# A hybrid decoder layer on one core: three PSUM banks for the projection thirds, lower rank for the exponentials, B and C loaded first

## The chip, the cores and the metric

The kernel runs on one core of one Trainium2 chip. The metric is device time in microseconds (us): the median of the runs shown. The profile is one further execution, taken by the hardware profiler.

## The reference, cut to what matters

One layer: a Mamba-2 (SSD) mixer and a Gated DeltaNet (GDN) mixer read the same projection, then an output projection and a SwiGLU block follow, for 1024 prompt tokens and 8 sequences of 8 new tokens. The change lies in the SSD part: 16 heads of 64 channels, two groups of B and C of 128 states, a decay matrix of exponentials per head, and a gate silu(z).

```python
proj = h @ w_in
z, xbc, dt_raw, qkv, gate, beta_raw, alpha_raw = jnp.split(proj, ...)
xbc = jax.nn.silu(_causal_dwconv(xbc, ...))            # x, B, C
...
acs = jnp.cumsum(dtc * A, axis=2)
seg = acs[:, :, :, None] - acs[:, :, None, :]
decay_ls = jnp.exp(jnp.where(causal, seg, -jnp.inf))    # one matrix per head and chunk
cb = jnp.einsum("bclgn,bcsgn->bclsg", Cc, Bc)           # per group
y_diag = jnp.einsum("bclsgr,bcsgrp->bclgrp", cb[..., None] * decay_ls, xdt)
...                                                     # states from chunk to chunk, y_off
y = y + ssd_D[:, None] * xs
y = y * silu(z)                                         # then a norm per group
```

## The kernel before, in words

TensorE (PE) multiplies fp32 as three passes over high and low halves: a weight tile of 128 columns is cast to `wh` (ACT, L164) and `wl` (DVE, L165), and `gemm` issues 8 steps of L189, L190, L191. The tokens (1024 + 64) are cut in three, so a weight tile needs three products, each in one PSUM bank: these are the *thirds* (`third`). Between the steps of a third, `gemm` calls `tick()`, which lets generators that stand in line issue a few PE instructions of other work. PE's order is thus written out by the program and kept; the order on the other engines is set by a scheduler, by priority, and each engine then works in that order.

After the GDN stage comes the SSD stage, at about 750 to 1012 us. PE runs there the thirds of z tiles and x tiles, and between them the SSD work: `ssd_group` once per group g (transposes of B by L670, products of B and C by L1006 into `cb`), and `ssd_pair` once for each pair j of heads, eight in all. A third's bank comes from the pool `ps_a` (two banks), everything else on PE takes banks of `ps_b` (six). ACT empties a third's bank: `evac` of `silu_tile` (L613, L615) into `sz` for z, `evac` of `conv_raw` (L566, L568) into `raw` for x. The next third but one takes the same bank and waits for that.

`decays(j)` makes the two decay matrices of pair j, one tile `L` a head: a DMA (L1033, on the queue of SP), a mask on POOL (L1037), a subtraction on DVE (L1039), and on ACT 9 exponentials a head (L1042 x8 and L1043), in place. `ssd_pair(j)` calls `decays(j + 1)`, so the exponentials of a pair are issued while the pair before it is worked on. Then DVE multiplies `L` by `cb` (L1057), and PE uses it (L1106, L1145). In a pair DVE carries the state `hS` through the chunks (L1099), PE multiplies it by C (L1116), and ACT copies PSUM results that PE reads soon after (`hS`, L1109 and L1131) and scales the old states (`h0`, L1150). L593 is the Silu of an x tile. The Silu and the exponential need different tables on ACT, so a change from one to the other shows as ACT_TABLE_LOAD.

Before the first pair, `ssd_all` calls `decays(0)` and then `ssd_group(0)`, which loads `bT` (a tile of the name `eb`) and `cT` from DRAM:

```python
def ssd_all():
    L = decays(0)
    for g in range(2):
        grp = yield from ssd_group(g)
```

Of the kernel before, what the change touches and what calls it, by code (L numbers as in the profile page):

```python
# [8 lines left out]
F32 = mybir.dt.float32  # L9
F32R = mybir.dt.float32r  # L10
BF16 = mybir.dt.bfloat16
AF = mybir.ActivationFunctionType
# [4 lines left out]
P = 128  # L17
D = 1024
KD = D // P
NP = 1024  # L20
NS = 64
T = NP + NS
NB = 8
TS = 8
NC = NP // P
# [18 lines left out]
def hybrid_step(ctx: ExitStack, tc: tile.TileContext, x_p, x_s, c_p, c_s, st_ssd, st_ssdc, st_gdn, st_gdnc,  # L44
# [4 lines left out]
    pe, act, dve, pool, sp = nc.tensor, nc.scalar, nc.vector, nc.gpsimd, nc.sync  # L49
# [10 lines left out]
    ps_a = ctx.enter_context(tc.tile_pool(name="ps_a", bufs=2, space=PSUM))  # L60
    ph_q = ExitStack()
    ps_b = ph_q.enter_context(tc.tile_pool(name="ps_b", bufs=6, space=PSUM))
# [67 lines left out]
    def tick():  # L130
        clock[0] += 1
        for t in list(tasks):
            if next(t, tasks) is tasks:
                tasks.remove(t)

    def spawn(gen):
        tasks.append(gen)
# [5 lines left out]
    def wait(n):  # L143
        for _ in range(n):
            yield
# [11 lines left out]
    def bank():  # L157
        return bg[0].tile([P, 512], F32, name="ps")
# [26 lines left out]
    def gemm(out, wt, xh, xl):  # L185

        hi, lo = wt
        for k in range(KD):
            pe.matmul(out, lhsT=hi[k], rhs=xh[k], start=(k == 0), stop=False)  # L189
            pe.matmul(out, lhsT=hi[k], rhs=xl[k], start=False, stop=False)  # L190
            pe.matmul(out, lhsT=lo[k], rhs=xh[k], start=False, stop=(k == KD - 1))  # L191
            if k in (2, 5, 7):
                tick()
# [29 lines left out]
    bias = init.tile([P, 512], F32, name="bias")  # L223
# [7 lines left out]
    ps = bank()  # L231
# [218 lines left out]
    neg = cA.tile([P, NT, 24], F32, name="neg")  # L450
# [98 lines left out]
    for t in lcs:  # L549
        pool.memset(t, 0.0)  # L550

    def third(wt, g, evac):
        t0, n = TH[g]
        while g not in hid_box:
            tick()
        ps = ps_a.tile([P, 512], F32, name="ps")
        gemm(ps[:, 0:n], wt, [h[:, t0:t0 + n] for h in hh], [h[:, t0:t0 + n] for h in hl])
        evac(ps, t0, n, min(n, NP - t0))

# [12 lines left out]
    def conv_tile(wt, ti, taps, bias, dst, dp, ds_, ch, done=None):  # L572
# [3 lines left out]
        if done is None:  # L576
            for g in range(3):
                third(wt, g, evac)
# [32 lines left out]
    def silu_tile(wt, dst_p, dst_s):  # L611
        def evac(ps, t0, n, m):
            act.activation(out=dst_p[:, t0:t0 + m], in_=ps[:, 0:m], func=AF.Silu)  # L613
            if m < n:
                act.activation(out=dst_s, in_=ps[:, m:n], func=AF.Silu)  # L615

        for g in range(3):
            third(wt, g, evac)
# [39 lines left out]
            if i < 15:  # L658
                w4 = load(i + 1)


    pools = {}

    def four(t, a):
        return [t[:, (4 * a + i) * P:(4 * a + i + 1) * P] for i in range(4)]

    def flip4(srcs):
        ps = bank()
        for i, t in enumerate(srcs):
            pe.transpose(ps[:, i * P:(i + 1) * P], t, ident)  # L670
        return ps.rearrange("p (c n) -> p c n", n=P)
# [224 lines left out]
    def first_two(wts):  # L896

        raws = [conv_raw() for _ in wts]
        for ps, raw in zip(first_ps, raws):
            raw[2](ps, *TH[0], TH[0][1])  # L900
        for g in range(1, 3):
            for wt, raw in zip(wts, raws):
                third(wt, g, raw[2])
        ph_0.close()
        spawn(rates_done())
        for (_, run), raw in zip(pair, raws):
            run(None, raw)
# [76 lines left out]
    sqp = ph_c.enter_context(tc.tile_pool(name="sqp", bufs=1, reuse_waits="tile"))  # L984
    cv = ph_a.enter_context(tc.tile_pool(name="cv2", bufs=2, reuse_waits="tile"))
    sd = ph_a.enter_context(tc.tile_pool(name="sd", bufs=1, reuse_waits="tile"))
    rsg = const.tile([P, 2, NT], F32, name="rsg")
    pool.memset(rsg, 0.0)

    def ssd_group(g):  # L990
        bT = sd.tile([P, T], F32, name="eb", bufs=2)
        sp.dma_start(out=bT, in_=bcdr[g * P:(g + 1) * P, :])
        cT = sd.tile([P, T], F32, name="cT")
        sp.dma_start(out=cT, in_=bcdr[(2 + g) * P:(3 + g) * P, :])
        yield from wait(9)
        btk = sd.tile([P, NT, P], F32, name="btk")
        cb = sd.tile([P, T], F32, name="cb")
        for a in range(2):
            act.copy(btk[:, 4 * a:4 * a + 4, :], flip4(four(bT, a)))
            yield  # L1000
        pool.memset(cb[64:128, NP:T], 0.0)
        for a in range(2):
            ps = bank()
            for i in range(4):
                c = 4 * a + i
                pe.matmul(ps[:, i * P:(i + 1) * P], lhsT=bT[:, c * P:(c + 1) * P], rhs=cT[:, c * P:(c + 1) * P],  # L1006
                          start=True, stop=True)
            dve.tensor_tensor(out=cb[:, 512 * a:512 * a + 512].rearrange("p (c n) -> p c n", n=P),
                              in0=ps.rearrange("p (c n) -> p c n", n=P),
                              in1=tri.unsqueeze(1).to_broadcast([P, 4, P]), op=ALU.mult)  # L1010
            yield
        ps = bank()
        pe.matmul(ps[0:NS, 0:NS], lhsT=bT[:, NP:T], rhs=cT[:, NP:T], start=True, stop=True)
        pe.matmul(ps[0:NS, P:2 * P], lhsT=bT[:, NP:T], rhs=ident, start=True, stop=True)
        dve.tensor_tensor(out=cb[0:NS, NP:T], in0=ps[0:NS, 0:NS], in1=tri8[:, 0:NS], op=ALU.mult)
        act.copy(btk[0:NS, NC, :], ps[0:NS, P:2 * P])
        bb = sd.tile([NS, NB, P], F32, name="bb")
        dve.tensor_tensor(out=bb, in0=btk[0:NS, NC, :].unsqueeze(1).to_broadcast([NS, NB, P]),
                          in1=blkm.unsqueeze(2).to_broadcast([NS, NB, P]), op=ALU.mult)

        cz = halT[:, 12:22, :].rearrange("p i n -> p (i n)")[:, 0:224].rearrange("p (i n) -> p i n", n=56)
        pool.memset(cz, 0.0)
        for a in range(2):
            act.copy(cz[:, :, 32 * a:32 * a + TS],
                     cT[:, NP + 32 * a:NP + 32 * a + 32].rearrange("p (b t) -> p b t", t=TS))
        return cT, btk, cb, bb, cz

    def decays(j):

        L = []  # L1030
        for h in (2 * j, 2 * j + 1):
            t = sd.tile([P, T], F32, name="L", bufs=4)
            sp.dma_start(out=t, in_=accr[h, 0:T].partition_broadcast(P))  # L1033
            L.append(t)
        for h, t in zip((2 * j, 2 * j + 1), L):
            tc_ = t[:, 0:NP].rearrange("p (c n) -> p c n", n=P)
            pool.affine_select(out=tc_, in_=tc_, pattern=[[0, NC], [1, P]], compare_op=ALU.is_ge, fill=-1e30, base=0,  # L1037
                               channel_multiplier=-1)
            dve.tensor_scalar(out=t[:, NP:T], in0=t[:, NP:T], scalar1=acs[:, NC, h:h + 1], scalar2=0.0,  # L1039
                              op0=ALU.subtract, op1=ALU.min)  # L1040
            for c in range(NC):
                act.activation(out=tc_[:, c, :], in_=tc_[:, c, :], func=AF.Exp, bias=neg[:, c, h:h + 1])  # L1042
            act.activation(out=t[:, NP:T], in_=t[:, NP:T], func=AF.Exp)  # L1043
        return L

    def ssd_pair(j, L, grp, sqs):
        cT, btk, cb, bb, cz = grp
# [5 lines left out]
        sp.dma_start(out=h0, in_=st_ssd[0, :, 2 * j:2 * j + 2].rearrange("b h p n -> (h p) b n"))  # L1053
        box = sbox[j]
        box["next"] = decays(j + 1) if j + 1 < KD else None
        for t in L:
            dve.tensor_tensor(out=t, in0=t, in1=cb, op=ALU.mult)  # L1057
# [116 lines left out]
    def group_norm(g, sqs):  # L1174
        yield from wait(6)
        ps = bank()
        for c in range(NT):
            n = P if c < NC else NS
            pe.matmul(ps[0:n, c:c + 1], lhsT=sqs[:, c * P:c * P + n], rhs=ones[:, 0:1], start=True, stop=True)
        rsqrt_small(rsg[:, g, 0:NC], ps[:, 0:NC], 1.0 / 512, EPS)  # L1180
        rsqrt_small(rsg[0:NS, g, NC:NT], ps[0:NS, NC:NT], 1.0 / 512, EPS)
        if g == 1:
            rate_box["norm"] = clock[0]

    def ssd_all():
        L = decays(0)
        for g in range(2):
            grp = yield from ssd_group(g)
            sqs = sqp.tile([P, T], F32, name="sqs")
            for j in range(4 * g, 4 * g + 4):  # L1190
                yield from ssd_pair(j, L, grp, sqs)
                pairs[0] = j + 1
                L = sbox[j]["next"]
            spawn(group_norm(g, sqs))

    def run_z(j):
# [6 lines left out]
        return f  # L1203

    ssd_run = ssd_all()
    spawn(ssd_run)
    jobs = []
# [698 lines left out]
```

## Time and profile before

| | |
|---|---|
| median of 3 runs | 2038.79 us (2030.85 to 2044.51) |
| profiled execution, own time | 2044.61 us |
| its span | 2042.9 us |
| PE busy | 1967.6 us, 96% |
| DVE, ACT busy | 66%, 49% |
| mean granted clock of PE | 0.981 |

The span runs from the first to the last instruction of the profiled execution; 1.7 us of its time lie around it. PE is nearly always busy, so a change shows in the time by what it takes from, or adds to, PE's idle time and its stretches at the lower granted clock.

### The profile page before, as it was taken

Reading aid. Unit: us, or ns where it says so; the run is one execution under the profiler, and the core shown is the slowest. Engines: PE = TensorE matmul, PEld = TensorE weight load, DVE = VectorE, ACT = ScalarE, POOL = GpSimd, SP = SyncE. Lnnn points to the kernel's source line nnn. Section 1 sums busy time; section 2 is a strip of 40 time slices with the busy share of each in tenths; the row PEclk is TensorE's granted clock in tenths of the full one; section 3 lists DMA queues with packets and bytes.
Section 4 is the critical chain, followed back from the end, with each engine's and each line's share of the span. In section 5 each row is a group of like instructions: output and inputs, shape, how many; then the busy total and the mean of one; then the engine's idle time right before and its main releaser. Section 6 shows DMA issues by size and latency. Waiting matters only on the chain. (4 is left out here: it accounts for less than half of the span.)

```text
span 2042.9 us, 35462 instructions
## 1 busy us (share of the span) xinstructions
PE 1967.6 (96%) x13211; PEld 1766.5 (86%) x13211; DVE 1356.1 (66%) x2949; ACT 1009.6 (49%) x2511; POOL 136.3 (7%) x188
## 2 busy tenths in 40 slices
PE   6999999999999998999989999999999999999998
PEld 4888989999999998899856667899999999988886
DVE  4668777876887655767637777885555556645465
ACT  3545454655555446756423556753333334544454
POOL 2100000000000001010002210100000000000000
PEclk8899999999999999999989999999999999999999
DMA  9123332333221236545266856422222223643131
GB/s 306 44 63 98 92 103 89 109 96 101 83 57 56 67 98 185 158 125 153 93 207 187 260 176 223 135 79 75 80 74 78 76 80 111 223 143 109 49 99 49
DMA packets 224764, 239.49 MB, mean 117 GB/s; under 512 B 19128, under 2 KB 177387, under 8 KB 224461
## 3 DMA queue, kind: packets, MB, share of 16 engines
q1 hardware_dynamic: 218203, 231.88, 36.6%
q10 hardware_dynamic: 6386, 5.33, 0.8%
q8 instruction: 104, 1.70, 0.3%
q14 instruction: 71, 0.58, 0.1%
HBM read 190.93 MB, written 46.25 MB: 116 GB/s over the span
## 5 line engine op out<-in xcount | busy, mean ns | idle before, releaser
L189 PE MATMUL ps<-hh,wh 128*128 128x384 f32 (+1 forms) x1232 | 439.4, 357 | 7.2 <-ACT raw L568 3.0
L190 PE MATMUL ps<-hl,wh 128*128 128x384 f32 (+1 forms) x1232 | 405.9, 329 | 0.0
L191 PE MATMUL ps<-hh,wl 128*128 128x384 f32 (+1 forms) x1232 | 405.9, 329 | 0.0
L1327 PE MATMUL ps<-wh,sh 128*128 128x512 f32 x678 | 276.0, 407 | 7.7 <-ACT wh L164 7.0
L1330 PE MATMUL ps<-wl,sh 128*128 128x512 f32 x678 | 268.3, 396 | 4.7 <-DVE wl L165 4.6
L189 PEld LDWEIGHTS ps<-hh,wh 128*128 128x128 f32 x1232 | 234.1, 190 | 25.3 <-issue 10.4
L1329 PE MATMUL ps<-wh,sl 128*128 128x512 f32 x604 | 240.1, 398 | 0.0
L190 PEld LDWEIGHTS ps<-hl,wh 128*128 128x128 f32 x1232 | 234.4, 190 | 0.8
L191 PEld LDWEIGHTS ps<-hh,wl 128*128 128x128 f32 x1232 | 233.2, 189 | 0.0
L164 ACT CAST wh<-wr 128x512 fp32r<-128x512 f32 x200 | 123.7, 621 | 186.5 <-PE ps L190 90.5
L165 DVE TENSOR_TENSOR wl<-wr,wh 128x512 fp32r<-128x512 f32 x200 | 136.6, 687 | 65.5 <-ACT wh L164 64.9
L1327 PEld LDWEIGHTS ps<-wh,sh 128*128 128x128 f32 x678 | 129.0, 190 | 49.8 <-issue 12.3
L165 DVE TENSOR_TENSOR wl<-wd,wh 128x512 fp32r<-128x512 f32 x130 | 89.6, 692 | 117.5 <-ACT wh L164 114.2
L1330 PEld LDWEIGHTS ps<-wl,sh 128*128 128x128 f32 x678 | 129.1, 190 | 35.6 <-DVE wl L165 6.9
L164 ACT CAST wh<-wd 128x512 fp32r<-128x512 f32 x130 | 80.7, 621 | 138.4 <-PE ps L1329 100.5
L1329 PEld LDWEIGHTS ps<-wh,sl 128*128 128x128 f32 x604 | 115.5, 191 | 21.3
L1807 PE MATMUL ps<-T_0h,wh 128*128 128x272 f32 x352 | 103.5, 294 | 3.1 <-DVE u L1823 1.8
L1809 PE MATMUL ps<-T_0h,wl 128*128 128x272 f32 x352 | 103.4, 294 | 0.7 <-DVE wl L1745 0.7
L1744 ACT CAST wh<-s 128x512 fp32r<-128x512 f32 x104 | 64.3, 620 | 79.5 <-PE ps L1808 73.8
L1807 PE MATMUL ps<-T_1h,wh 128*128 128x272 f32 x352 | 102.2, 290 | 0.5 <-ACT as L1814 0.5
L1808 PE MATMUL ps<-T_0l,wh 128*128 128x272 f32 x352 | 102.7, 292 | 0.0
L1809 PE MATMUL ps<-T_1h,wl 128*128 128x272 f32 x352 | 101.6, 289 | 0.0
(490 smaller groups left out, 4383.3 us busy)
## 6 DMA issues: line engine op xcount, KB each, us to landing
wr<-in_w_in_dram SPq DMA_DIRECT2D x104, 256.0 KB
wr<-in_w_gate_up_dram SPq DMA_DIRECT2D x104, 256.0 KB
wr<-in_w_out_dram SPq DMA_DIRECT2D x96, 256.0 KB
w<-in_w_ada_dram SPq DMA_DIRECT2D x16, 1024.0 KB
wd<-in_w_down_dram SPq DMA_DIRECT2D x22, 512.0 KB
actdr<-as SPq DMA_DIRECT2D x18, 544.0 KB
L<-accr SPq DMA_DIRECT2D x16, 544.0 KB
am<-actdr SPq DMA_DIRECT2D x44, 192.0 KB
```

Source lines behind the costliest of these rows:

```text
L164: act.copy(wh, src)
L165: low.tensor_tensor(out=wl, in0=src, in1=wh.bitcast(F32), op=ALU.subtract)
L189: pe.matmul(out, lhsT=hi[k], rhs=xh[k], start=(k == 0), stop=False)
L190: pe.matmul(out, lhsT=hi[k], rhs=xl[k], start=False, stop=False)
L191: pe.matmul(out, lhsT=lo[k], rhs=xh[k], start=False, stop=(k == KD - 1))
L1327: pe.matmul(o, lhsT=sh[:, cs], rhs=wh, start=first, stop=False)
L1329: pe.matmul(o, lhsT=sl[:, cs], rhs=wh, start=False, stop=False)
L1330: pe.matmul(o, lhsT=sh[:, cs], rhs=wl, start=False, stop=last)
L1744: act.copy(wh, opa[p])
L1807: pe.matmul(o, lhsT=wh[:, cs], rhs=bh[:, m, :], start=(m == 0 and not on), stop=False, **on)
L1808: pe.matmul(o, lhsT=wh[:, cs], rhs=bl[:, m, :], start=False, stop=False, **on)
L1809: pe.matmul(o, lhsT=wl[:, cs], rhs=bh[:, m, :], start=False, stop=(m == 3), **on)
```

## The change

Three edits, all in the SSD stage. (1) `third` counts its calls, and once the SSD pools exist every third call takes its bank from `ps_b`. (2) The exponentials of `decays(j)` for j > 0 are issued at a lower priority: 40 lower for the first head of a pair, 120 lower for the second. (3) The loads of `bT` and `cT` become a function, `load_bc`; for group 0 it is called ahead of `decays(0)`. `pools` only moves up. All lines below shift by 3 to 8: L613 becomes L616, L615 L618, L566 L569, L568 L571, L593 L596, L1042 L1048, L1043 L1049, L1109 L1115, L1131 L1137.

```diff
+    pools, thirds = {}, [0]
+
     def third(wt, g, evac):
         t0, n = TH[g]
         while g not in hid_box:
             tick()
-        ps = ps_a.tile([P, 512], F32, name="ps")
+        thirds[0] += 1
+        ps = (ps_b if "ssd" in pools and thirds[0] % 3 == 0 else ps_a).tile([P, 512], F32, name="ps")
         gemm(ps[:, 0:n], wt, [h[:, t0:t0 + n] for h in hh], [h[:, t0:t0 + n] for h in hl])
         evac(ps, t0, n, min(n, NP - t0))
...
     sd = ph_a.enter_context(tc.tile_pool(name="sd", bufs=1, reuse_waits="tile"))
+    pools["ssd"] = sd
...
-    def ssd_group(g):
+    def load_bc(g):
         bT = sd.tile([P, T], F32, name="eb", bufs=2)
         sp.dma_start(out=bT, in_=bcdr[g * P:(g + 1) * P, :])
         cT = sd.tile([P, T], F32, name="cT")
         sp.dma_start(out=cT, in_=bcdr[(2 + g) * P:(3 + g) * P, :])
+        return bT, cT
+
+    def ssd_group(bT, cT):
         yield from wait(9)
...
-            for c in range(NC):
-                act.activation(out=tc_[:, c, :], in_=tc_[:, c, :], func=AF.Exp, bias=neg[:, c, h:h + 1])
-            act.activation(out=t[:, NP:T], in_=t[:, NP:T], func=AF.Exp)
+            with tc.high_priority(-(40 + 80 * (h % 2)) if j else 0):
+                for c in range(NC):
+                    act.activation(out=tc_[:, c, :], in_=tc_[:, c, :], func=AF.Exp, bias=neg[:, c, h:h + 1])
+                act.activation(out=t[:, NP:T], in_=t[:, NP:T], func=AF.Exp)
         return L
...
     def ssd_all():
-        L = decays(0)
         for g in range(2):
-            grp = yield from ssd_group(g)
+            bc = load_bc(g)
+            if g == 0:
+                L = decays(0)
+            grp = yield from ssd_group(*bc)
```

PE and POOL keep their order. On the queue of SP the two loads go ahead of the two first `L`, as the diff shows, and one weight load later moves by a place. What else moves is on ACT, and behind it on DVE. Three places follow.

ACT, at the start of the stage, while pair 0 begins: `ps_8836`, `ps_8883` and `ps_8983` are the three thirds of one z tile, read into `sz_8835`; `L_8924` and `L_8926` are the decay matrices of pair 1, heads 0 and 1. Before:

```order
L999 COPY btk_8846<-ps_8863 128x512
L613 ACTIVATE sz_8835<-ps_8836 128x384
L1024 COPY halT_124<-cT_8732 128x4x8 x2
L1016 COPY btk_8846<-ps_8908 64x128
L1042 ACT_TABLE_LOAD
L1042 ACTIVATE L_8924<-L_8924,neg_644 128x128 x8
L1043 ACTIVATE L_8924<-L_8924 128x64
L1042 ACTIVATE L_8926<-L_8926,neg_644 128x128 x8
L1043 ACTIVATE L_8926<-L_8926 128x64
L613 ACT_TABLE_LOAD
L613 ACTIVATE sz_8835<-ps_8883 128x384
L613 ACTIVATE sz_8835<-ps_8983 128x256
```

And now:

```order
L616 ACT_TABLE_LOAD
L616 ACTIVATE sz_8835<-ps_8836 128x384
L1021 COPY btk_8846<-ps_8908 64x128
L616 ACTIVATE sz_8835<-ps_8883 128x384
L164 CAST wh_9012<-wr_9010 128x512
L1049 ACT_TABLE_LOAD
L1049 ACTIVATE L_8924<-L_8924 128x64
L1048 ACTIVATE L_8924<-L_8924,neg_644 128x128 x8
L616 ACT_TABLE_LOAD
L616 ACTIVATE sz_8835<-ps_8983 128x256
L618 ACTIVATE sz_8835<-ps_8983 128x64
```

The reading of `ps_8883` has moved ahead of all exponentials of pair 1, that of `ps_8983` ahead of the second head's, and there is one table load more.

ACT, at the end of pair 2: `ps_9711` is the last third of an x tile, read into `raw_9572`; `L_9766` and `L_9768` belong to pair 4. Before:

```order
L164 CAST wh_9842<-wr_9840 128x512
L1171 ACTIVATE sz_9301<-y_9599 128x1088
L1042 ACT_TABLE_LOAD
L1042 ACTIVATE L_9766<-L_9766,neg_644 128x128 x8
L1043 ACTIVATE L_9766<-L_9766 128x64
L1042 ACTIVATE L_9768<-L_9768,neg_644 128x128 x8
L1043 ACTIVATE L_9768<-L_9768 128x64
L566 COPY raw_9572<-ps_9711 128x256
L568 COPY raw_9572<-ps_9711 128x8x8
```

And now:

```order
L164 CAST wh_9842<-wr_9840 128x512
L1177 ACTIVATE sz_9301<-y_9599 128x1088
L569 COPY raw_9572<-ps_9711 128x256
L571 COPY raw_9572<-ps_9711 128x8x8
L586 ACTIVATE xs_9827<-raw_9572,prm1T_122 128x1024
L588 ACTIVATE xs_9827<-raw_9572,prm1T_122 128x64
L600 COPY lc0_646<-raw_9572 128x3
L601 COPY lc0_646<-raw_9572 128x24
L164 CAST wh_9848<-wr_9846 128x512
L1048 ACTIVATE L_9766<-L_9766,neg_644 128x128 x8
```

The two copies from the bank have moved ahead of the exponentials of pair 4.

ACT, in pair 5: `hS_10760` and `hS_10792` are copies that PE reads, `L_10559` a matrix of the pair after, `xs_10638` an x tile under its Silu. Before:

```order
L164 CAST wh_10659<-wr_10657 128x512
L1109 COPY hS_10706<-ps_10707 128x512
L613 ACT_TABLE_LOAD
L613 ACTIVATE sz_10663<-ps_10664 128x384
L1150 ACTIVATE h0_10555<-h0_10555,eb_10552 128x128
L1122 COPY y_10683<-ps_10697 128x128
L1150 ACTIVATE h0_10555<-h0_10555,eb_10552 128x128 x7
L1109 COPY hS_10760<-ps_10761 128x512
L1131 COPY hS_10792<-ps_10783 128x128
L593 ACTIVATE xs_10638<-xs_10638 128x1024
```

And now:

```order
L1048 ACTIVATE L_10559<-L_10559,neg_644 128x128
L1128 COPY y_10683<-ps_10697 128x128
L1048 ACTIVATE L_10559<-L_10559,neg_644 128x128 x3
L1049 ACTIVATE L_10559<-L_10559 128x64
L1156 ACTIVATE h0_10555<-h0_10555,eb_10552 128x128 x7
L1115 COPY hS_10760<-ps_10761 128x512
L596 ACT_TABLE_LOAD
L596 ACTIVATE xs_10638<-xs_10638 128x1024
L597 ACTIVATE xs_10638<-xs_10638 128x64
L1137 COPY hS_10792<-ps_10783 128x128
```

Exponentials now stand among the pair's own work, and a table load and the Silu of `xs` have come between the two copies.

## Rows read from the trace of the kernel before

**Rows 1.** The page's first part: busy time of each engine, whole span.

```profile
PE 1967.6 (96%) x13211; PEld 1766.5 (86%) x13211; DVE 1356.1 (66%) x2949; ACT 1009.6 (49%) x2511; POOL 136.3 (7%) x188
```

**Rows 2.** Waits of PE, 750 to 1012 us: total, times, longest, in us.

```profile
PE ps L189 <- ACT raw L568: 3.0, 1, 3.0
PE ps L670 <- DMA eb<-bcdr: 3.0, 1, 3.0
PE ps L189 <- ACT sz L613: 2.8, 2, 2.6
PE ps L189 <- ACT sz L615: 1.3, 1, 1.3
```

**Rows 3.** Timeline of PE around three stops: start, length, instruction, idle before it.

```profile
768.67 0.66 PE L670 MATMUL ps<-ident,eb 128*128 128x128 f32 x4 [3.00 <-DMA eb<-bcdr]
...
773.82 1.05 PE L1006 MATMUL ps<-cT,eb 128*128 128x128 f32 x8
...
788.22 0.44 PE L189 MATMUL ps<-hh,wh 128*128 128x384 f32 x1 [2.62 <-ACT sz L613]
...
790.90 0.33 PE L1106 MATMUL ps<-L,xd 128*64 128x128 f32 x2
...
861.20 0.34 PE L190 MATMUL ps<-hl,wh 128*128 128x384 f32 x1
861.38 0.34 PE L191 MATMUL ps<-hh,wl 128*128 128x384 f32 x1
864.73 0.45 PE L189 MATMUL ps<-hh,wh 128*128 128x384 f32 x1 [3.02 <-ACT raw L568]
...
866.08 0.52 PE L191 MATMUL ps<-hh,wl 128*128 128x384 f32 x1
866.40 0.52 PE L189 MATMUL ps<-hh,wh 128*128 128x384 f32 x1
```

**Rows 4.** Busy time (count) by window: PE, PEld, DVE, ACT, POOL; clock; DMA share.

```profile
768.60:773.20 4.60, 4.53 (x20) 4.43 (x21) 0.00 (x0) 4.57 (x13) 0.00 (x0) 0.63 1.05 296
...
788.20:798.00 9.80, 9.78 (x85) 9.19 (x86) 5.86 (x19) 3.79 (x11) 0.00 (x0) 1.00 0.20 55
...
864.70:868.50 3.80, 3.77 (x15) 3.77 (x16) 1.89 (x2) 3.77 (x7) 0.00 (x0) 0.58 0.18 54
...
750.00:1010.00 260.00, 249.86 (x1831) 229.79 (x1830) 175.93 (x358) 158.69 (x393) 21.15 (x25) 0.99 0.47 139
```

**Rows 5.** Timeline of ACT ahead of the stops that end at 788.22 and 864.73.

```profile
780.00 1.28 ACT L1042 ACT_TABLE_LOAD   x1
781.29 2.45 ACT L1042 ACTIVATE L<-L,neg 128x128 f32<-128x128 f32 x8
...
786.39 1.28 ACT L613 ACT_TABLE_LOAD   x1
787.68 0.77 ACT L613 ACTIVATE sz<-ps 128x384 f32<-128x384 f32 x2
...
864.22 0.35 ACT L566 COPY raw<-ps 128x256 f32<-128x256 f32 x1
```

**Rows 6.** Timeline of SP's queue: the first loads of the stage.

```profile
760.46 1.66 SPq L1033 DMA_DIRECT2D L<-accr  x2
762.17 0.42 SPq L992 DMA_DIRECT2D eb<-bcdr  x1
```

**Rows 7.** Timeline of DVE: the first work on each of the two first `L`.

```profile
764.51 1.18 DVE L1039 TENSOR_SCALAR L<-L,rate 128x64 f32<-128x64 f32 x1 [0.95 <-DMA L<-accr]
767.36 1.19 DVE L1039 TENSOR_SCALAR L<-L,rate 128x64 f32<-128x64 f32 x1 [1.67 <-DMA L<-accr]
```

**Rows 8.** Timeline of ACT and of DVE inside pairs 5 and 2.

```profile
951.48 0.27 ACT L1131 COPY hS<-ps 128x128 f32<-128x128 f32 x1 [0.74 <-PE ps L1128]
951.64 1.06 ACT L593 ACTIVATE xs<-xs 128x1024 f32<-128x1024 f32 x1
...
846.50 1.62 DVE L1099 SCALAR_TENSOR_TENSOR hS<-hS,rate,ps 128x64 f32<-128x64 f32 x8 [1.32 <-PE ps L1085]
```

More of the change, by code (lines that the diff above doesn't have):

```diff
@@ L659, in ada_rest @@
                 w4 = load(i + 1)
-    pools = {}
     def four(t, a):
```

## The prediction

> **What bounds the kernel now.** I read the page's first part first: PE is busy for 1967.6 us, 96%, while DVE stands at 66% and ACT at 49% [rows 1]. So an edit on ACT or on a queue is worth only what it takes out of PE's idle time, or out of its time at the lower clock. The edits touch one stage, 750 to 1012 us, so the second view is the list of PE's waits there [rows 2]. It holds four lines: 3.0 us for a copy into `raw`, 3.0 us for the load of `eb` (this is `bT`), 2.8 us in two waits for a Silu into `sz`, 1.3 us for another. Together that is 10.1 us, and it is all that PE waits there by the trace. The window of the whole stage bounds it from the other side: PE is busy for 249.86 of 260 us [rows 4], which leaves 10.1 us too.
>
> The third view is PE's timeline around the stops [rows 3], and beside it the granted clock [rows 4]. After the stops that end at 768.67 and at 864.73 the chip grants 0.63 of full speed over 4.6 us and 0.58 over 3.8 us, a mix of its two levels, 2.4 and 1.2 GHz. In PE's rows this is a start every 0.32 us (866.08, 866.40) where it had been one every 0.18 us (861.20, 861.38). After the stop that ends at 788.22, 2.62 us long, the clock stays at 1.00. The lost time is 4.6 x (1 - 0.63) = 1.7 us and 3.8 x (1 - 0.58) = 1.6 us, together 3.3 us. A stop that goes takes its slow stretch with it, so the **ceiling** of the change is 10.1 + 3.3 = 13.4 us, 0.7% of the time.
>
> The fourth view tells whose work stands in front [rows 5]. Ahead of the stop that ends at 788.22, ACT has loaded the table for the exponential (1.28 us), done two heads (2.45 us for eight), and loaded the table back (1.28 us), before it reads the bank at 787.68. Ahead of the stop that ends at 864.73 it does the same two heads of another pair, as the order at the second place shows, and copies the bank only at 864.22. In both cases PE had ended its third and needed the bank but one.
>
> **Part by part.** *Three banks.* With two banks a third waits for the reading of the third before the last; with three, every third third starts in a bank that has long been free, and the others wait for one read earlier. Following the bank of each third through the order after, the ones that start behind the stops for `sz` and `raw` take banks that were last read before the exponentials in front of them, or that DVE had read well before. The Silu waits (2.8 and 1.3) and the `raw` wait (3.0) go by this alone: 7.1 us, with the 1.6 us of clock behind 864.73. The price would be an SSD step that finds one of its six banks still held by a third. Those steps come at the earliest some microseconds after ACT's reading; I put it at nothing, and the cover is ACT's promptness: if a reading comes late, PE waits at the SSD step for the same copy.
>
> *Lower rank.* It takes the same waits from the other side, since copies now go ahead of the exponentials of the next pair (the order at the first and second places). So the first two edits overlap, and their gain counts once. What rank does alone is to move exponentials into the pair's own work. They are needed only a pair later: those of pair 1 begin at 781.29 before [rows 5], while PE first reads even pair 0's at 790.90 [rows 3], so their own lateness costs little at first. The cost lies in ACT's order, which is fixed: a copy that PE waits for directly can now stand behind a table load and exponentials. Before, no such wait shows in this stage in any line of [rows 2], so one place at a time has to be bounded. At least 0 (the exponentials fit into a gap of ACT, which is busy for only 158.69 of 260 us [rows 4]), and at most a table load and a head, 1.28 + 2.45 = 3.7 us [rows 5], in each of seven pairs: 26 us. By place: in pair 5 the copy into `hS` that began at 951.48 now stands behind a table load and the Silu that came after it (1.28 + 1.06 = 2.3 us) [rows 5, 8]; I take half, about 1.2 us, since the copy waited 0.74 us for PE anyway and PE reads it some time after its end. In pair 2 the second head's exponentials end, by adding their lengths up in ACT's gaps, near 846; DVE's product with `cb` follows, and the eight updates of the state that began at 846.50 [rows 8] move behind it: about 1.0 us. In pair 3 about 0.3 us, in the others nothing. Sum 2.5 us, near the lower end since most places have a gap in front.
>
> The change adds four table loads on ACT. By the row one takes 1.28 us, and the next activation starts 0.01 us after its end (781.29 behind 780.00 + 1.28) [rows 5]: 4 x 1.28 = 5.1 us of ACT, of an idle time of 260 - 158.69 = 101 us in the stage. I count it inside the places above and nowhere else. The Trainium skill, page "ScalarE: Activation LUTs", section "What ACT_TABLE_LOAD costs", speaks against this edit: it gives a switch of tables about 2.66 us, the load of 1283 ns and a drain of some 1380 ns. By it the four would be an estimated 10.6 us of ACT. The trace agrees on the load; no row here shows a drain behind it.
>
> *B and C first.* PE stops for 3.00 us, up to 768.67, for `bT`, the third load in the queue, issued at 762.17 behind the two `L` [rows 3, 6]. The first two landed at 764.5 and 767.3 by the work that DVE starts on them [rows 7]. Now `bT` is first and `cT` second, in the same slots and of the same size, so they should land at 764.5 and 767.3. PE wants `bT` at 768.67 - 3.00 = 765.7: no wait, by a margin of 1 us. Without the stop and the slow stretch it wants `cT` 4.7 us earlier than the 773.82 at which it multiplied by it [rows 3], at 769.1: a margin of 1.8 us. The gain is 3.0 + 1.7 = 4.7 us. The price is that the two `L` of pair 0 land about two loads later, by an estimate from `bT`'s 768.67 as third near 768.7 and 771. Their exponentials take twice 2.45 us and a table load [rows 5], so they end near 778, and DVE's product of the second head near 780. PE reads them first at 790.90, or near 783.6 without the stops up to there (3.00 + 1.7 + 2.62): some 3 us of slack. What is late next is the reading of a z third behind these exponentials (the table load and `ps_8836` at the first place), near 778; the third that takes its bank is the one that starts at 788.22 before, near 781 without the stops.
>
> **The sum.** 7.1 + 1.6 + 4.7 = 13.4 us, less 2.5 us: **11 us**. The profiled execution of 2044.61 us, span 2042.9 and 1.7 around it, would become 2033.6. It lies 5.8 us above the median of the runs, so I take the gain off the median: 2038.79 - 11 = **2028 us**. Behind the stage PE's order is the same, and the queues there wait for events of PE and DVE that come earlier with it, so the gain is kept.
>
> **The rivals.** *Most of it eaten on ACT.* The four table loads all stand in front of copies that PE waits for: 4 x 1.28 = 5.1 us more, so 13.4 - 2.5 - 5.1 = 6 us, **2033**. For it: ACT's order is fixed, and pair 5 shows the pattern. Against: ACT idles 101 us in the stage. By the page's price the four cost 10.6, and with 2.5 the gain would be nothing, **2038.5**; no row bears that out, and I give it 0.03 apart from the above.
>
> *Slower.* The copies of `hS` that PE reads at once stand behind a table load and a head's exponentials in every pair: 3.7 us x 7 = 26 us, less 13.4: +12.6 us, **2051**. It decides from 13.4 / 7 = 1.9 us a pair on. For it: the exponentials now run among the pair's own steps, where DVE, ACT and PE hand work to each other with waits under 1 us. Against: at seven places out of seven a whole head would have to start just ahead of a copy; the order shows the exponentials split around the copies, and only one place with a load between two of them.
>
> *It does nothing.* `bT` lands no earlier since the weight and state loads share the DMA engines (busy share 1.05 behind 768.6 [rows 4]), and a third stops for another reading: gain under 2 us, **2038**. Against: the first load in the queue had landed 4 us after its issue.
>
> *More than expected.* Without stops the clock stays up in places that I don't count, or the stage's end meets less idle time behind it: over 20 us, under 2018. No row in the stage has that much to give.
>
> **Chances.** Forecast (gain of 7 to 14 us) 0.62, eaten on ACT 0.17, the page's price 0.03, nothing 0.06, slower 0.06, more 0.06. The range holds the forecast, the eaten gain and the case of nothing, and on either side some 5 us for the runs themselves, which spread by 14 us before: 2017 to 2042. A measurement of this kernel tells about 1% (20 us) from no change, and the ceiling is 0.7%, so: faster by over 1% 0.06, within 1% 0.89, slower by over 1% 0.05 (the slower case, with its price nearly doubled or unlucky runs).
>
> **What would show it.** In the profile after, PE's list of waits between 750 and 1012 should have lost the lines of `raw`, `eb` and `sz`, and the window around 768 and 865 should show a clock of 1.00. New lines of PE waiting for `hS` or DVE waiting for `L` should sum to 2 to 3 us. If `eb` is still there, the step on the landing of the first load is wrong; if a third still waits for `sz` or `raw`, the step on the banks; if PE waits for `hS` in most pairs, the price of the rank was too low. The stage's end, near 1012 us before, should come some 11 us earlier, and PE's busy time be less by the 3.3 us of slow clock.

## The result, and the profile after

The changed kernel takes 2021.78 us, median of 10 runs (2017.53 to 2033.8), against 2037.61 (2030.85 to 2050.06) for the kernel before: a ratio of 0.9922, 95% interval 0.9906 to 0.9937, so some 16 us less (13 to 19). A second comparison, on another occasion (run c1 below), gave 0.9935 (0.991 to 0.996), 13 us. The forecast was 11 us and 2028, in a range of 2017 to 2042.

The profiled execution after has a span of 2015.8 us. PE is busy for 97% of it, 96% before [rows 1], and for 16.3 us less:

```profile
PE 1951.3 (97%) x13211; PEld 1752.5 (87%) x13211; DVE 1356.6 (67%) x2949; ACT 1014.1 (50%) x2515; POOL 138.7 (7%) x188
```

Only 2.0 of these 16.3 us are in the stage (271.4 us before and 269.4 after). 10.0 lie ahead of it, in code that is the same, and are clock: the mean granted clock up to the stage is 0.97 in the trace before and 0.99 in this one. So the busy time that the forecast named as a sign can't be read from these two traces.

PE's waits after, 750 to 1012 us (total, times, longest), answer to [rows 2]:

```profile
PE ps L1091 <- DVE xe L1074: 3.0, 1, 3.0
PE ps L1286 <- POOL rsg L122: 0.9, 1, 0.9
PE ps L1141 <- ACT hS L1137: 0.9, 2, 0.7
PE ps L1122 <- DVE hS L1105: 0.2, 1, 0.2
```

All four lines of before are gone: `raw`, `eb` and both of `sz`. (The wait for `rsg` lies behind the pairs, in the part that the stage's end has moved into the window.) In their place stands one that no step of the forecast has: 3.0 us for `xe`. PE's timeline after shows the stop, and the windows what the clock did behind it (columns as in [rows 4]):

```profile
773.31 0.34 PE L191 MATMUL ps<-hh,wl 128*128 128x384 f32 x1
776.66 1.14 PE L1091 MATMUL ps<-xe,btk 128*128 128x128 f32 x8 [3.02 <-DVE xe L1074]
```

```profile
756.00:762.00 6.00, 6.00 (x42) 5.92 (x41) 0.91 (x3) 1.96 (x7) 0.27 (x1) 1.00 0.91 288
...
776.60:782.00 5.40, 5.34 (x35) 4.91 (x36) 5.37 (x15) 5.35 (x14) 1.09 (x1) 0.68 0.54 145
848.00:852.00 4.00, 4.00 (x37) 3.71 (x36) 4.00 (x8) 3.95 (x10) 0.07 (x1) 1.00 0.89 283
...
750.00:1010.00 260.00, 255.77 (x1882) 232.58 (x1881) 183.49 (x372) 168.07 (x408) 23.15 (x26) 0.99 0.52 153
```

The first window is where PE multiplies by `bT` now, the third where it used to stop for `raw`: full clock in both, where [rows 4] have 0.63 and 0.58. The second is the stretch behind the new stop, at 0.68: 5.4 x 0.32 = 1.7 us more. So of the 3.3 us of clock in the forecast's ceiling this trace kept half.

PE runs the same instructions in the same order in both kernels, so the lead of one trace over the other can be read at each of them (its start before less its start after). Between the products that stand at 760 and at 784 us before, the lead grows by 4.9 us (the stop for `bT` with its slow stretch); over the stop that ended at 788.22 it grows by 2.8; between 788 and 800 it falls by 4.7 (the new stop); then come 1.6 for the second Silu wait and 4.9 for the `raw` wait with its slow stretch; between 950 and 990 it falls by 1.6. Over the stage that makes 8.2 us in these two traces.

The lead over the whole execution, 27.1 us, is not all the change's: 8.3 us of it are there before the stage begins, in code that is the same. The runs below give such a split for every kernel.

### The profile page after: what moved, and what is told of

Its sections match the earlier page's. It is cut to its first block, busy times and chain, and to the rows that moved or that the text cites. A ratio compares the mean times of both kernels' runs of the same rounds, so it can differ in the third digit from the quotient of the medians.

```text
span 2015.8 us, 35469 instructions
## 1 busy us (share of the span) xinstructions
PE 1951.3 (97%) x13211; PEld 1752.5 (87%) x13211; DVE 1356.6 (67%) x2949; ACT 1014.1 (50%) x2515; POOL 138.7 (7%) x188
## 4 chain that ended last, share of the span: by engine, by line
PE 79%; DVE 9%; DMA 6%; ACT 3%; issue 2%; POOL 0%; SPq 0%; DVEq 0%; POOLq 0%; ACTq 0%
PE ps L189 8%; PE ps L190 8%; PE ps L191 8%; PE ps L1815 7%; PE ps L1817 7%; PE ps L1816 7%; PE ps L1335 7%; PE ps L1338 6%; PE ps L1337 6%; PE ps L671 2%; PE ps L725 1%; DMA L<-accr 1%; DVE tm L827 1%; DVE rr L829 1%; DMA mx<-mixdr 1%
## 5 line engine op out<-in xcount | busy, mean ns | idle before, releaser
L1337 PEld LDWEIGHTS ps<-wh,sl 128*128 128x128 f32 x604 | 114.7, 190 | 21.3
```

The source lines that it names most:

```text
L1337: pe.matmul(o, lhsT=sl[:, cs], rhs=wh, start=False, stop=False)
```

## The experiments

All are compared with the kernel before. Beside each ratio, what the stage took in the trace: from the start of one given product to that of another (at 733.5 and 1015.2 us in the first trace of before), and what the execution had before these and after them, up to the end of its last product.

```
kernel                                   ratio (95%)             before it  stage  after it
before, first trace                                                  733.5  281.7  1020.7
c0  before again                         1.0004 (0.9985-1.0023)      725.3  285.5  1016.0
the change                               0.9922 (0.9906-0.9937)      725.2  273.5  1010.0
c1  the change again                     0.9935 (0.991-0.996)        731.8  272.2  1017.4
e1  three banks only                     0.9943 (0.9919-0.9967)      731.4  276.5  1015.6
e2  lower rank only                      0.9932 (0.9908-0.9956)      731.9  275.0  1014.9
e3  B and C first only                   0.9978 (0.9961-0.9995)      730.1  278.9  1016.6
e6  rank, B and C first                  0.9959 (0.9941-0.9977)      725.6  277.4  1010.6
e5  banks, B and C first                 0.9916 (0.9896-0.9936)      730.5  269.6  1010.7
c2  e5 again                             0.9929 (0.9913-0.9944)      726.1  274.5  1015.7
e4  change, subtraction ranked lower     0.9912 (0.989-0.9934)       726.7  271.3  1015.9
e9  e5, subtraction ranked lower         0.9927 (0.9908-0.9945)      732.7  268.9  1016.1
e7  change, L of pair 1 loaded earlier   0.9907 (0.9892-0.9923)      725.3  269.4  1015.3
e8  e5, L of pair 1 loaded earlier       0.9906 (0.9885-0.9928)      725.0  268.5  1015.0
```

The columns beside the stage spread by 8.5 and 10.7 us between traces, without regard to the edits. The stage's own column sorts by them better and is read first below, but two traces of one program differ there too, by 3.8 us (before), 1.3 (the change) and 4.9 (e5 and c2). A stage by itself is known to some 2 us, and differences of 1 or 2 us between kernels show nothing.

Part of that spread is the clock. Summed over the stage (length times one less the granted clock), the time lost to it is 3.4 us in the first trace before and 6.8 in c0; 1.7 in both traces of the change, in e5, c2 and e9; 3.4 in e1, e2 and e6; 5.1 in e3; nothing in e4, e7 and e8. Not every slow stretch follows a stop. Here are c1 and the first trace before over the same products, with no wait of PE near by:

```profile
882.70:886.10 3.40, 3.40 (x13) 3.31 (x12) 1.17 (x1) 2.70 (x7) 1.71 (x2) 0.50 0.22 64
```

```profile
896.70:900.10 3.40, 3.40 (x23) 3.36 (x23) 1.78 (x5) 2.62 (x8) 2.58 (x2) 1.00 0.33 87
```

The granted clock falls to 0.50 at this place (the lower of its two levels, 1.2 GHz) in c0, c1, e1, e3, e5, e6 and e9 and stays up in the other seven traces, whatever the edits; it costs up to 1.7 us. Nor does every stop have one: in c0 a slow stretch follows the stop that [rows 4] show at full clock.

**The two controls.** c0 is the kernel before, unedited.

> The kernel before once more, to see by a second trace how much its own executions differ outside the stage. The stage from 760 to 1012 us should show the same four waits of PE, 10 us in all, whatever the time. In the first trace what follows the stage took about 5 us longer than in three of the four variants, whose code is the same there. If that was chance, it is gone in this trace; if it stays, the variants gain something behind the stage too. Ratio 1.000.

Ratio 1.0004. The four waits are there, but that for `eb` is 4.1 us in place of 3.0, and the stage takes 3.8 us more than in the first trace; what follows it takes 4.7 less. Beside the longer wait it is the two more slow stretches (3.4 us) that make c0's stage the longer one. So the stage before is 283.6 us, give or take 2, and the 5 us behind it were largely chance.

c1 is the changed kernel, unedited.

> The changed kernel once more: ratio 0.992 again. In its stage PE waits 3 us for xe again (the cause is in the order and in the loads), and the stage is some 8 us shorter than in the kernel before. What follows the stage, 10.6 us shorter than before in the first pair of traces, comes out 4 to 6 us shorter, or less, if that was chance.

The stage takes 272.2 us, 11.4 less than the mean of the two of before (10.1 in the first trace of the change). The wait for `xe` is 1.2 us and not the 3.0 expected, with the same program and no slow stretch behind it: the stop depends on when a load lands, not on the order alone.

```profile
PE ps L1091 <- DVE xe L1074: 1.2, 1, 1.2
```

What follows the stage is 3 us shorter than in the first trace of before, and 1.4 longer than in the second: the 10.6 us were chance for the most part.

**One edit at a time.** e1 has the banks alone:

```diff
+    pools, thirds = {}, [0]
...
+        thirds[0] += 1
+        ps = (ps_b if "ssd" in pools and thirds[0] % 3 == 0 else ps_a).tile([P, 512], F32, name="ps")
...
+    pools["ssd"] = sd
```

> The three banks alone, without the lower rank and without B and C first. By my theory (the waits for sz and raw go by the banks alone) PE's list of waits from 750 to 1012 us loses the lines of sz (2.8 and 1.3 us) and raw (3.0), keeps the 3.0 of eb, and the clock behind the raw wait (1.6) comes back: 8.7 us less than before, a ratio of 0.9957. The rival (the rank does it, a third bank only moves the wait to a later third, as the exponentials still stand in front of the copy) has at least 4 us of waits for sz and raw left and a gain of under 4 us, 0.998 or more.

e2 has the rank alone:

```diff
+            with tc.high_priority(-(40 + 80 * (h % 2)) if j else 0):
                 for c in range(NC):
                     act.activation(out=tc_[:, c, :], in_=tc_[:, c, :], func=AF.Exp, bias=neg[:, c, h:h + 1])
                 act.activation(out=t[:, NP:T], in_=t[:, NP:T], func=AF.Exp)
```

> The lower rank alone, with two banks and with the old order of loads. By my theory the copies out of the banks go ahead of the exponentials, so the waits for sz and raw go as they do with three banks, against 2.5 us of new waits for hS and L: 6 us less than before, 0.997. The rival (with two banks a third still starts before ACT has come to the copy, and the additional table loads stand in front of it) gives a gain of under 2 us, or a loss: 0.999 to 1.002.

PE's waits in the stage, of e1 and then of e2 (L671 is L670 of before; line numbers move by 1 to 8 in the changed kernel, not by 3 to 8):

```profile
PE ps L671 <- DMA eb<-bcdr: 4.1, 1, 4.1
PE ps L1121 <- DVE hS L1104: 1.1, 2, 0.6
PE ps L1140 <- ACT hS L1136: 0.2, 1, 0.2
```

```profile
PE ps L671 <- DMA eb<-bcdr: 3.5, 1, 3.5
PE ps L1141 <- ACT hS L1137: 0.9, 2, 0.7
PE ps L189 <- ACT sz L616: 0.2, 1, 0.2
```

Each edit by itself takes away the waits for `sz` and `raw`, but for 0.2 us: the stage is 7.1 us (banks) and 8.6 us (rank) shorter than before. Both rivals fall. The two gains are the same one, as the forecast had it. (By its ratio e2 gained more than the 6 us expected, 0.9932 against 0.997; part of that is the excess over the stage that is taken up below.) Without the rank PE waits for the state `hS` instead, which no step had: in e1 1.1 us, in pairs 0 and 2. The rank's price in PE's waits is 0.7 us, for the copy in pair 5; the other 0.2 of that line are at 1013.6 us in the trace before as well, just outside [rows 2].

e3 has the loads alone, with `ssd_group(g)` split into `load_bc(g)` and the rest as in the diff of the change:

```diff
     def ssd_all():
-        L = decays(0)
         for g in range(2):
-            grp = yield from ssd_group(g)
+            bc = load_bc(g)
+            if g == 0:
+                L = decays(0)
+            grp = yield from ssd_group(*bc)
```

> B and C first alone. By the sum on record the stop for eb and its slow stretch go: 4.7 us, 0.9977. The rival comes from the trace after the change: without that stop the loads of the pair after next go out earlier and share the DMA engines with the matrices L of pair 1, DVE waits for these ahead of xe, and PE for xe (3.0 us and about 1.7 of clock): gain of 0 to 1 us, 1.000 to 0.9995, with a line of PE waiting for xe in its place.

```profile
PE ps L189 <- ACT raw L571: 3.0, 1, 3.0
PE ps L189 <- ACT sz L616: 1.2, 2, 1.0
PE ps L189 <- ACT sz L618: 1.2, 1, 1.2
PE ps L1090 <- DVE xe L1073: 0.9, 1, 0.9
```

The wait for `eb` is gone and the stage 4.7 us shorter. That it is just the term of the sum is partly chance: in PE's waits e3 saves the 3.0 us and another 1.7 of the Silu waits (2.4 in place of 4.1), pays 0.9 for `xe`, and loses more to the clock than the first trace before (5.1 and 3.4 us). Its ratio, 0.9978, is the one expected. The rival has its wait too, 0.9 us for `xe`, but not its price.

**Two edits at a time.** e6 leaves out the banks (its edit: `ps = ps_a.tile(...)` as before), e5 the rank (the exponentials without `tc.high_priority`).

> The change without the third bank: lower rank, B and C first. Since the rank alone took away the waits for sz and raw, the banks add nothing by the first theory: as the changed kernel, 0.992, with the wait for xe (3.0 us) in it. The rival (the change needs both, since without the stop for B a third starts sooner) has a wait for sz of 1 to 3 us, 0.993 to 0.994.

> The change without the lower rank: three banks, B and C first. By the sum on record the rank adds no gain where the banks are there, and costs 2.5 us: this kernel would be 1 to 2.5 us faster than the changed one, 0.991. The rival (the exponentials at their old rank stand in front of copies that a third soon needs, and three banks give less room once PE no longer stops for B) has waits for sz or raw back, some 2 us or more: 0.993 to 0.995.

PE's waits in e6:

```profile
PE ps L189 <- ACT sz L616: 2.4, 2, 2.2
PE ps L1091 <- DVE xe L1074: 2.3, 1, 2.3
PE ps L1141 <- ACT hS L1137: 0.9, 2, 0.7
PE ps L1122 <- DVE hS L1105: 0.4, 2, 0.2
```

Here the rival holds: once PE no longer stops for `bT`, the rank alone doesn't save the Silu wait, since that third now comes while pair 0's exponentials, which keep their rank, are on ACT. This is the place that the prediction named under "what is late next"; it had some 3 us of room there, and without the third bank there was none. The banks are needed, by the trace and by the ratio (0.9959, a smaller gain than either case expected). The rank isn't: e5's stage takes 269.6 us, 3.3 less than the mean of the change's two, with 0.7 us of waits in all. But c2, the same kernel again, had the stop for `xe`:

> The change without the lower rank once more, beside the two that build on it: 0.9916 again by the theory that the rank costs 2 us and adds nothing; 0.993 if its advantage over the changed kernel was chance.

```profile
PE ps L1090 <- DVE xe L1073: 4.2, 1, 4.2
PE ps L1121 <- DVE hS L1104: 1.0, 1, 1.0
PE ps L1140 <- ACT hS L1136: 0.2, 1, 0.2
```

So that stop belongs to the loads, not to the rank, and comes and goes between 0 and 4.2 us in one and the same program. e5's lead over the change was chance, then: whether the rank costs time on the whole is within the intervals (0.9916 and 0.9929 without it, 0.9922 and 0.9935 with it).

**What the new stop is.** In the changed kernel, SP's queue issues the loads of the start of the stage like this:

```profile
752.14 0.35 SPq L994 DMA_DIRECT2D eb<-bcdr  x1
...
757.45 6.53 SPq L1038 DMA_DIRECT2D L<-accr  x2
765.92 1.09 SPq L1057 DMA_DIRECT2D eb<-eaccr  x2
767.06 1.21 SPq L1059 DMA_DIRECT2D h<-in_state_ssd_dram  x1
```

and DVE works in this order:

```profile
770.78 1.22 DVE L1023 TENSOR_TENSOR bb<-btk,blkm 64x1024 f32<-64x1024 f32 x1
774.74 1.18 DVE L1044 TENSOR_SCALAR L<-L,rate 128x64 f32<-128x64 f32 x1 [2.75 <-DMA L<-accr]
775.84 0.68 DVE L1074 TENSOR_TENSOR xe<-ps,rate 128x512 f32<-128x512 f32 x1
```

The subtraction (L1044) works on the `L` of pair 1, which nobody needs yet, and stands ahead of `xe` of pair 0, which PE wants at 773.5. The `L` was handed to the queue from 757.45 on and landed at 774.7. Behind it come pair 1's `eb` and `h0` at 765.92: before, the queue issued them at 779.46, as the slot of `eb` comes free when PE has used `bT`:

```profile
779.46 1.09 SPq L1051 DMA_DIRECT2D eb<-eaccr  x2
```

While the `L` is on its way the DMA engines are busy throughout, at a share of 1.08 and 1.14 in two windows:

```profile
768.70:772.00 3.30, 3.30 (x24) 3.30 (x24) 3.25 (x4) 2.91 (x6) 0.00 (x0) 1.00 1.08 289
773.50:776.60 3.10, 0.14 (x1) 0.00 (x0) 1.86 (x3) 1.80 (x4) 1.09 (x1) 1.00 1.14 213
```

e4 tries DVE's order, e7 the loads. e4 is the whole change and

```diff
-            dve.tensor_scalar(out=t[:, NP:T], in0=t[:, NP:T], scalar1=acs[:, NC, h:h + 1], scalar2=0.0,
-                              op0=ALU.subtract, op1=ALU.min)
+            with tc.high_priority(-100 if j else 0):
+                dve.tensor_scalar(out=t[:, NP:T], in0=t[:, NP:T], scalar1=acs[:, NC, h:h + 1], scalar2=0.0,
+                                  op0=ALU.subtract, op1=ALU.min)
```

> The whole change, and the subtraction that DVE makes on L (for j over 0) at a lower rank as well, so that on DVE it stands behind xd and xe of the pair before. If PE's new stop for xe (3.0 us at 773.5, and a slow stretch of 3.4 us at half clock behind it) comes from DVE's order alone, it goes: 4.7 us less than the changed kernel, some 2017, a ratio to before of 0.990. The rival (the DMA engines are the bound there: the late L is then late for the exponentials and for the product with cb, and PE stops for that) gives what the changed kernel gives, 0.992, with a wait for L or hS in place of that for xe.

```profile
PE ps L1123 <- DVE hS L1102: 1.3, 1, 1.3
PE ps L1142 <- ACT hS L1138: 0.9, 2, 0.7
PE ps L1135 <- ACT hS L1116: 0.7, 1, 0.7
```

The wait for `xe` is gone; the subtraction has moved only ahead of the first copy of the state (L1102), so the next step on DVE waits for the same load, 1.3 us. So the order does make the stop (here the `L` came 23.1 us behind the issue of `bT`, later than in the change's traces, and PE had `xe` in time), but the rival holds as well: the late load is met one step further on. Its stage is 271.3 us, 1.6 less than the change's, not 4.7, and that is no more than the slow stretch of 1.7 us that this trace doesn't have. e9 does the same by 300, in e5:

> Three banks, B and C first, the old rank of the exponentials, and only DVE's subtraction on L at a lower rank (by 300, behind the state's updates). If DVE's order is what turned a late L into a stop of PE, there is no wait for xe and none for the first hS: 0.990 to 0.992, as without the rank. The rival (the subtraction now comes so late that the exponential behind it holds up ACT, which works in order) gives a new wait for sz or hS on ACT and 0.993 to 0.995.

PE then waits for 0.2 us in the whole stage, which takes 268.9 us. As a test of the order this trace is weak: its `L` came 19.8 us behind the issue of `bT`, about as early as in e5, where PE didn't wait for `xe` in the old order either. Its ratio, 0.9927, is no better than e5's: this trace had 732.7 and 1016.1 us around the stage, the slow end of both columns. e7 is the whole change and

```diff
         hs = (2 * j, 2 * j + 1)
+        ahead = decays(1) if j == 0 else None
         eb = sd.tile([P, T], F32, name="eb", bufs=2)
...
-        box["next"] = decays(j + 1) if j + 1 < KD else None
+        box["next"] = ahead or (decays(j + 1) if j + 1 < KD else None)
```

> The whole change, and for pair 0 the two loads of the next pair's L go out ahead of the pair's own eb and h0 (816 KB less in front of them). If PE's stop for xe comes from L landing late behind other loads, L lands some 3 us or more earlier, DVE doesn't stop at its subtraction, and the wait for xe is gone: the stage some 2 to 4 us shorter than in the changed kernel's two traces, a ratio of 0.990 to 0.992. The rival (eb and h0, now later, are waited for instead, by DVE's product with eb or PE's transposes of h0) shows a new wait for these and the same time as the changed kernel, 0.993.

(What goes behind is 2 x 272 + 512 = 1056 KB; the expectation miscounted it.) SP's queue, DVE and PE's waits in e7:

```profile
752.21 0.36 SPq L994 DMA_DIRECT2D eb<-bcdr  x1
...
755.33 1.35 SPq L1038 DMA_DIRECT2D L<-accr  x2
756.73 1.45 SPq L1058 DMA_DIRECT2D eb<-eaccr  x2
```

```profile
766.58 1.17 DVE L1044 TENSOR_SCALAR L<-L,rate 128x64 f32<-128x64 f32 x1 [1.97 <-DMA L<-accr]
...
773.44 0.67 DVE L1075 TENSOR_TENSOR xe<-ps,rate 128x512 f32<-128x512 f32 x1
```

```profile
PE ps L1142 <- ACT hS L1138: 0.9, 2, 0.7
PE ps L1092 <- DVE xe L1075: 0.5, 1, 0.5
PE ps L1123 <- DVE hS L1106: 0.3, 1, 0.3
```

The first `L` of pair 1 lands by 766.6, 14.4 us behind the issue of `bT`, and not 22.6 as in the change; the wait for `xe` is 0.5 us, the stage 269.4 us, and no wait for `eb` or `h0` has come. So the late load behind DVE's order was the cause of the stop, by both ways of taking it out: order (e4) and landing (e7, and e8 below). The sizes agree. In the two traces of the change and in e5 and c2 PE is ready for `xe` 21.3 to 21.5 us behind the issue of `bT`, and where it stops, 1.9 us pass from the first work on the `L` (the mask, at 774.78 in the first trace) to PE's start on `xe` (776.66); so the stop should be the landing less some 19.6 us. The landings at 22.6, 20.8, 19.4 and 23.8 us give 3.0, 1.2, 0 and 4.2 us, which are the waits measured. What makes the `L` late is only argued: no run holds back pair 1's `eb` and `h0`, and in the eight traces with B and C first and the old place of that `L` they were issued 13.8 to 14.2 us behind `bT` throughout, while the `L` landed 19.4 to 24.7 us behind it. e8 is the same edit in e5, without the rank:

> Three banks, B and C first, the old rank of the exponentials, and L of pair 1 ahead of eb and h0: the version in which no known wait of the stage is left. If the waits add up as the traces say, PE waits for under 1 us in the stage and the time is that of the kernel without the rank or 1 us less: 0.990 to 0.992. The rival (the loads that went behind cost as much) 0.993.

```profile
PE ps L1122 <- DVE hS L1105: 1.0, 1, 1.0
PE ps L1141 <- ACT hS L1137: 0.2, 1, 0.2
```

Its stage of 268.5 us is the shortest, 15.1 less than before, and its median of 2018.25 us the lowest: 0.9906. It and e7 (0.9907, 2020.35 us) lie ahead of the change, but the intervals overlap with the change's.

## Why the prediction was right

The number lay in the range, and the direction was the one forecast; the gain of the two comparisons, 16 and 13 us, lies above the forecast case (7 to 14 us) and in it. The sum's gain was right, its loss consisted of other things than forecast, and that the two came out at nearly 11 us is partly luck.

*The gain.* Of the ceiling of 13.4 us (10.1 of idle time, 3.3 of clock), the leads of the trace show 4.9 for `bT` (forecast 4.7), 2.8 + 1.6 for the Silu waits (2.8 + 1.3), 4.9 for `raw` (3.0 + 1.6). The stops for `bT` and `raw` took their slow stretches with them, as the windows show; the new stop brought one of its own.

*One gain, not two.* The banks and the rank take away the same waits: e1 and e2 alone 7.1 and 8.6 us of stage. What I didn't see is that with B and C first the rank alone no longer does (e6, 2.4 us for `sz`). The price of the banks, put at nothing, was nothing by PE's waits: no line of PE's waits after is for the reading of a bank.

*The rank's price*, 2.5 us forecast. Pair 5 was right in place and mechanism, 0.7 us against 1.2. ACT after, in pair 5, and PE's product that reads the second copy:

```profile
932.16 0.56 ACT L1115 COPY hS<-ps 128x512 f32<-128x512 f32 x1
932.74 1.28 ACT L596 ACT_TABLE_LOAD   x1
934.03 1.06 ACT L596 ACTIVATE xs<-xs 128x1024 f32<-128x1024 f32 x1
...
935.14 0.25 ACT L1137 COPY hS<-ps 128x128 f32<-128x128 f32 x1
```

```profile
935.44 0.33 PE L1141 MATMUL ps<-ident,hS 128*128 128x128 f32 x1 [0.70 <-ACT hS L1137]
```

The terms for pairs 2 and 3 (1.0 and 0.3 us) were nothing: no line of PE's waits in the changed kernel lies there. In pair 2 it is rather the other way: e1, e5, c2 and e8, with the banks and without the rank, wait there for `hS`, 0.5 to 1.0 us. In all the lead falls by 1.6 us between 950 and 990 (1.8 in c1); 0.9 of it is pair 5, the rest lies around another wait for `hS` at 971.7 of before, 0.2 us (0.5 in c1), that no term has. The table load took 1.28 us again, and the activation began 0.01 us behind it; the drain of some 1380 ns that the Trainium skill counts into a switch (page "ScalarE: Activation LUTs", section "What ACT_TABLE_LOAD costs") shows in no row here either.

*The step that was missing.* "What is late next", for the loads, went as far as pair 0's `L` and the Silu reading behind it. It stopped short of pair 1: PE, no longer stopped, frees the slot of `eb` 13.5 us sooner by the issue times (779.46 less 765.92; 8.3 of them are the earlier start of the stage), pair 1's next loads join a queue that already keeps the DMA engines busy, and DVE sits in front of the subtraction. (That these loads are what delays the `L` isn't shown, as said above; that the late `L` makes the stop is.) That cost 4.7 us in the first trace and 1.8 in the second (1.3 by 800; 0.5 more by 838, around a wait of 0.3 us for a copy of `hS`), which together with the rank's 1.6 and 1.8 us stands against the 2.5 us of the forecast: 6.3 and 3.6 us, so the loss was up to two and a half times what the sum had. The second trace loses 1.4 us more near 897, where no stop is.

So the stage came out 10.1 and 11.4 us shorter against the mean of the two traces before: 10.7, by the sum 11. With one trace against one it is 8.2 to 13.3, so the near agreement is luck in part: the larger loss is made good in the mean by c0's longer stage, of which two slow stretches more are chance. The measured gain of 13 to 16 us is larger than that by 2 to 5. It isn't settled where the rest lies. Each run has its granted clock, and the time lost to it can be split off. In the 21 runs of before beside c1 it is 32.4 of 2037.3 us on average, in the six of c1 28.0 of 2023.7: of 13.6 us, 4.4 are clock and 9.2 are not. The stages of the traces have 3.4 and 7.5 us of these. So some of the rest may be clock and some idle time of PE, and neither part is clear of chance. The times of most variants show as much more than their stages (by the ratios, e1 11.6 of time and 7.1 of stage, e8 19 and 15.1), so it may lie behind the stage; but the twelve traces of the edits have from 1010.0 to 1017.4 us there and the two of before 1020.7 and 1016.0, with PE's order the same in all, and two traces of before are too few to tell.

The rivals: copies behind exponentials in every pair (2051 us) had no such place but one; the case in which the loads do nothing (gain under 2 us) has the wait for `eb` gone against it, and e3's ratio, whose interval (0.9961 to 0.9995) reaches down to a gain of 1 us. The four table loads as a price (2033, or 2038.5 at the higher price that the prediction gave beside it) didn't show either: with and without the rank the stage differs by 0.9 us where the late load is out of the way (e7 and e8). The case of more (under 2018) is not the measured one.

## What to carry to other kernels

When a stop of the busiest engine goes, ask what that engine's progress releases: here it freed a buffer's slot, and the next loads then went out while one was still on its way that came late. A small step on an in-order engine that works on data for later (the subtraction on the next pair's `L`) is a risk wherever it stands ahead of a step that is needed now; load its data earlier, or rank it behind. And where two edits aim at the same wait, run each alone and both pairs: here one of them was enough in one order of loads and not in the other.

## What I had not expected of the hardware

The same loads of the same program, issued in the same order, landed at quite different times: the mask on the first `L` of pair 1 began 22.6 us after the issue of `bT` in the first trace of the changed kernel and 20.8 in the second, 19.4 and 23.8 in the two of e5 and c2, and PE's stop went with it from 0 to 4.2 us. A margin of some 2 us against a landing in a stretch where the DMA engines are full is no margin. The spread isn't free of pattern. In the four traces with B and C first and the old place of that `L` that reach the stage by 727 us (the first of the change, c2, e4, e6) it landed 22.6 to 24.7 us behind, in the four that reach it from 730 us on (c1, e3, e5, e9) 19.4 to 20.8. Why is not shown; but an execution that comes to the stage sooner gives part of that lead back in it.
